# FFN up-projection of a hybrid attention layer: two blocks of one feature group through seven products instead of eight

## The chip, the core and the metric

The kernel runs on one NeuronCore of one Trainium2 chip. The metric is the device time of one execution in microseconds (us), the median of several runs. Five engines work side by side, each with its own in-order queue: TensorE (PE; its weight loads are the row PEld) multiplies, ScalarE (ACT) and VectorE (DVE) cast, copy and add, GpSimd (POOL) does small work, and SyncE (SP) issues the transfers from main memory. They are ordered by semaphores alone: an instruction waits for its operands, and everything queued behind it on its engine waits too.

## What is computed

One layer for 256 tokens of width 2048, in float32. After attention and the first LayerNorm the token matrix `x` (256 x 2048) is modulated by a vector that depends on the condition `c`, goes through a SwiGLU of hidden width 5632, and is added back:

```python
sh1, sc1, g1, sh2, sc2, g2 = ada_mods(c, w_ada, b_ada)          # c (1 x 2048) @ w_ada (2048 x 12288)
x = layer_norm(DN_ALPHA * x + g1 * (heads @ w_out), ln1_g, ln1_b)
u = x * (1.0 + sc2) + sh2
y = (silu(u @ w_gate) * (u @ w_up)) @ w_down                    # 2048 x 5632 twice, 5632 x 2048
x = layer_norm(DN_ALPHA * x + g2 * y, ln2_g, ln2_b)
```

The change lies in `u @ w_gate` and `u @ w_up`.

## The kernel before

**Precision.** A float32 product is made of three matmuls (`mm3`): every operand is split into a high part `hi` (a cast, on ACT) and a rest `lo` (a subtraction, on DVE), and hi\*hi + hi\*lo + lo\*hi is summed in a PSUM bank. Weights arrive in tiles `raw` of 128 partitions x 2048 (four 128-feature slices of 512 columns, 1 MiB), of which there are four (`RAW_BUFS`). Each raw is split in two **pieces** of 128 x 1024 (`hi` and `lo`, four buffers each, `HL_BUFS`); a piece normally feeds 12 matmuls (2 slices, 2 token tiles, 3 terms). A cast into a buffer waits until the piece four before it has been multiplied, so at most three pieces are ready ahead of TensorE.

**Blocks.** The 5632 hidden columns are 11 blocks `f` of 512. The features are four groups `g` of 512. Group 2 (features 1024 to 1535) of the gate columns of blocks 0 to 9 already goes through seven products instead of eight (the Winograd form of Strassen's scheme, `folded`): with half-matrices b11, b21 (one column block) and b12, b22 (the other), DVE forms b12-b11, b22-b12, b22-b11 and b21 of the last of these, and seven products of 6 matmuls each replace eight. A pair of blocks is the pair of columns there. Partial results are handed from bank to bank by ACT copies (`nc.scalar.copy(b, a)` and the like), since three sums share a beginning.

**First half.** The modulation vectors of the groups 1 to 3 need rows of `w_ada`. The kernel starts the FFN before they are there: `first_half` is a list of steps, one for each block, matrix (gate, up) and group, that a call of `project` makes: load a raw, split it, 24 matmuls into two banks. Blocks 0 to 2 do group 0 alone, blocks 3 to 9 groups 0 and 1; when both are in, ACT copies the two banks to SBUF (`spills[f]`). Beside these steps runs `side`, the sums over `w_ada` for groups 2 and 3: 16 steps, each loading 1 MiB of `w_ada` into a raw of the same four and adding it up with two DVE instructions (`adav`, L466). At the end of each group DVE transposes and folds the sum (`flip`, `fold`), TensorE multiplies it by a small matrix (`grp`, L1160), and DVE copies the answer out (`sh`, `sc`). `merge` spreads the 16 side steps evenly over the 25 steps of the list. After the list `z_part` makes the features 1024 to 2047 of `u` (`u2h`, `u2l`), and the second half begins. Outside a small region the order of instructions on each engine is set when the kernel is built, by the program's order and a scheduler.

Of the kernel before, what the change touches and what calls it, by code (L numbers as in the profile page):

```python
# [13 lines left out]
F32 = mybir.dt.float32  # L14
F32R = mybir.dt.float32r
# [251 lines left out]
def dit_layer(ctx: ExitStack, tc: tile.TileContext, x, c, cx, c_ctx, w_ada, b_ada, w_in, q_norm_g,  # L267
# [12 lines left out]
    def acc_bank():  # L280
        return acc_ps.tile([P, NB], F32, tag="acc", name="acc")

    def wk_bank():
        return wk_ps.tile([P, NB], F32, tag="wk", name="wk")

    def run(steps):
        for s in steps:
            s()

    def merge(*lists):  # L290

# [1171 lines left out]
    u2h = pb.tile([P, KD, SEQ], F32R, tag="u2h", name="u2h")  # L1463
    u2l = pb.tile([P, KD, SEQ], F32R, tag="u2l", name="u2l")
    rests = {(t, kk): pb.tile([P, 2, SEQ], F32, tag="t2k", name="uf2", bufs=4)[:, :, :P] for t in range(NT) for kk in (0, 2)}
    hTh = [pb.tile([P, 4, SEQ], F32R, tag=f"hTh{f}", name="hTh") if f < KF // 4 - SPLIT_F else None for f in range(KF // 4)]
    hTl = [pb.tile([P, 4, SEQ], F32R, tag=f"hTl{f}", name="hTl") if f < KF // 4 - SPLIT_F else None for f in range(KF // 4)]

    def z_part(kk, uf=None):
        ps = wk_bank()  # L1470
        for j in range(2):
            for t in range(NT):
                nc.tensor.transpose(ps[:, (j * 2 + t) * P : (j * 2 + t + 1) * P],
                                    xt[:, t, (kk + j) * P : (kk + j + 1) * P], ident)
# [27 lines left out]
    def sums(a11, a21, a12, a22):  # L1502

        tt = nc.vector.tensor_tensor
        tt(a22, a21, a22, op=ALU.add)
        tt(a21, a11, a21, op=ALU.subtract)
        tt(a11, a22, a11, op=ALU.subtract)
        tt(a12, a12, a11, op=ALU.subtract)

    def form_tiles():  # L1510
        return [pb.tile([P, 2, SEQ], F32R, tag="t2k", name=name, bufs=4) for name in ("fh", "fl")]

    def plain(forms, h, l, k0):
        for m, (t, k) in {11: (0, k0), 12: (0, k0 + 2), 22: (1, k0 + 2)}.items():
            forms[m] = [tuple(u[:, k + j, t * P : (t + 1) * P] for u in (h, l)) for j in range(2)]
        return forms

    def token_forms(v1, v2, k0):

        forms = {}  # L1520
        sums(v1[:, :, :P], v1[:, :, P:], v2[:, :, :P], v2[:, :, P:])
        for lr, x in (((2, 3), v1), ((4, 1), v2)):
            hi, lo = form_tiles()
            split(hi, lo, x)
            for i, m in enumerate(lr):
                forms[m] = [(hi[:, j, i * P : (i + 1) * P], lo[:, j, i * P : (i + 1) * P]) for j in range(2)]
        return plain(forms, u2h, u2l, k0)
# [10 lines left out]
                forms[m] = [(hi[:, j, i * P : (i + 1) * P], lo[:, j, i * P : (i + 1) * P]) for j in range(2)]  # L1538
        return plain(forms, hTh[f], hTl[f], 0)

    def folded(columns, forms, shared):


        def products(ps, m, piece, first):
            w = split_raw(piece)
            for j in range(2):
                mm3(ps, *forms[m][j], w[j], first and j == 0, j == 1, not first)

        half = 2 * NB
        r1, r2 = (load_raw(w_, k0, G4, c0, NB) for w_, k0, c0 in columns)  # L1550
        b11, b21, b12, b22 = r1[:, :half], r1[:, half:], r2[:, :half], r2[:, half:]
        a, e = wk_bank(), wk_bank()
        tt = nc.vector.tensor_tensor
        products(a, 11, b11, True)
        b = acc_bank()
        nc.scalar.copy(b, a)
        tt(b11, b12, b11, op=ALU.subtract)
        yield
        products(e, 1, b11, True)
        tt(b12, b22, b12, op=ALU.subtract)  # L1560
        tt(b11, b22, b11, op=ALU.subtract)
# [76 lines left out]


    groups = [1 if f < ONE_F else EARLY_G if f < SPLIT_F else 0 for f in range(FFN // NB)]  # L1640
    spills, first_half = [], []
    for f in range(SPLIT_F):
        spills.append([pb.tile([P, NT, NB], F32, tag=f"hT{c}{KF // 4 - SPLIT_F + f}", name="spill") for c in "hl"])
        for i, w_ in enumerate((w_gate, w_up)):
            st = {}

            def step(g, f=f, i=i, w_=w_, st=st):
                if g == 0:
                    st["accs"] = [acc_bank() for _ in range(NT)]
                project(st["accs"], w_, f, g, 0, groups[f] * 4 - 1)  # L1650
                if g == groups[f] - 1:
                    for t in range(NT):
                        nc.scalar.copy(spills[f][i][:, t, :], st["accs"][t])

            first_half += [lambda g=g, step=step: step(g) for g in range(groups[f])]
    late_sums = [lambda: vector_sums(2 * NB), lambda: pb.tile([P, 2 * NB], F32, tag="lgb", name="adav")]
    scales = ada_vector_steps((4 * D + NB,), NB, lambda: late_sums[1]()[:, :NB], second_scales)
    side = sum((second_modulation(g, late_sums[g - EARLY_G]) for g in range(EARLY_G, ng)), [])
# [78 lines left out]
    for f0 in range(0, SPLIT_F, 2):  # L1737
# [248 lines left out]
```

## Time and profile before

| | |
|---|---|
| Device time, three runs | 1122.33, 1124.48, 1124.83 us (median 1124.48) |
| Profiled execution: span from the first to the last instruction | 1121.0 us (its own device time is not given beside the span; the runs' median is 3.5 us above it) |
| PE busy | 1102.3 us, 98% of the span |
| DVE busy | 903.4 us, 81% |
| ACT busy | 598.7 us, 53% |
| DMA engines | about 82% of the span, 287 GB/s on average |

A busy share is the time in which the engine had an instruction in flight. Matmuls overlap, so a PE that is 100% busy is read by the distance of the starts of two matmuls and not by the length of one.

### The profile page before, as it was taken

The page shows a single profiled execution, that of the slowest core. Times are in us where ns is not written, and L with a number is a line of the kernel's source. Part 1 is how long each engine was busy: PE and PEld are TensorE (multiplying, and loading weights), DVE is VectorE, ACT ScalarE, POOL GpSimd, SP SyncE. Part 2 cuts the span into 40 slices and gives each one's busy share as a digit, 9 for nine tenths or more (in the row PEclk, how much of TensorE's full clock was granted, in tenths as well). Part 3 has the DMA queues.
Part 4 walks back from the last instruction along what each step waited for, and adds up shares of the span by engine and source line. Part 5 has one row for each costly group of instructions (what it writes and reads, how often), then busy time and mean ns, then how long its engine had stood idle before and what let it go on. Part 6 is the DMA issues. An engine that isn't in the chain of part 4 may idle for free.

```text
span 1121.0 us, 14130 instructions
## 1 busy us (share of the span) xinstructions
PE 1102.3 (98%) x5213; PEld 883.7 (79%) x5213; DVE 903.4 (81%) x1133; ACT 598.7 (53%) x875; POOL 36.7 (3%) x82
## 2 busy tenths in 40 slices
PE   8999999999999999999999999999999999999995
PEld 6766688777887788888888878888888888888884
DVE  5763589899999888787778697988996987689876
ACT  3341554878685356444475565767766344444442
POOL 1000030110100001000000000000000000000000
PEclk9999999999999999999999999999999999999998
DMA  9999999778999778999956677777776998669742
GB/s 321 394 385 375 393 362 377 247 234 274 345 332 395 249 269 321 348 318 296 336 182 216 223 220 266 234 246 271 228 267 216 329 348 293 228 235 379 287 149 76
DMA packets 178317, 321.26 MB, mean 287 GB/s; under 512 B 8732, under 2 KB 43196, under 8 KB 175943
## 3 DMA queue, kind: packets, MB, share of 16 engines
q1 hardware_dynamic: 177528, 320.03, 81.7%
q8 instruction: 41, 0.67, 0.2%
q10 hardware_dynamic: 720, 0.33, 0.1%
q14 instruction: 28, 0.23, 0.1%
HBM read 304.07 MB, written 16.25 MB: 286 GB/s over the span
## 4 chain that ended last, share of the span: by engine, by line
PE 91%; DMA 3%; DVE 2%; ACT 1%; SPq 1%; issue 0%; ACTq 0%; DVEq 0%
PE acc L341 20%; PE acc L343 20%; PE acc L342 20%; PE wk L342 8%; PE wk L341 8%; PE wk L343 8%; PE wk L1081 2%; PE wk L654 2%; DMA raw<-in_w_in_dram 2%; DVE lo L332 1%; DMA lgb<-in_ln_g_dram 1%; PE wk L755 1%; SPq L569 1%; DMA xt<-in_x_dram 0%; PE wk L1414 0%
## 5 line engine op out<-in xcount | busy, mean ns | idle before, releaser
L331 ACT CAST hi<-raw 128x1024 fp32r<-128x1024 f32 x279 | 290.7, 1054 | 256.4 <-PE acc L343 162.4
L332 DVE TENSOR_TENSOR lo<-raw,hi 128x1024 fp32r<-128x1024 f32 x279 | 336.1, 1220 | 103.6 <-ACT hi L331 101.4
L341 PE MATMUL acc<-hi,u2h 128*128 128x512 f32 x390 | 152.5, 391 | 0.0
L343 PE MATMUL acc<-hi,u2l 128*128 128x512 f32 x390 | 151.7, 390 | 0.7 <-DVE u2l L1669 0.7
L342 PE MATMUL acc<-lo,u2h 128*128 128x512 f32 x390 | 151.8, 389 | 0.0
L603 ACT CAST hi<-raw 128x1024 fp32r<-128x1024 f32 (+1 forms) x86 | 87.4, 1030 | 113.8 <-DMA raw<-in_w_in_dram 63.2
L466 DVE SCALAR_TENSOR_TENSOR adav<-raw,cs,adav 128x512 f32<-128x512 f32 (+1 forms) x128 | 121.4, 949 | 8.4 <-DMA raw<-in_w_ada_dram 4.9
L606 DVE TENSOR_TENSOR lo<-raw,hi 128x1024 fp32r<-128x1024 f32 (+1 forms) x86 | 101.3, 1194 | 16.3 <-ACT hi L603 15.5
L341 PE MATMUL acc<-hi,uh 128*128 128x512 f32 x256 | 103.7, 405 | 1.3 <-ACT uh L769 0.8
L342 PE MATMUL wk<-lo,u2h 128*128 128x512 f32 x264 | 103.1, 390 | 0.5 <-DVE lo L332 0.5
L343 PE MATMUL wk<-hi,u2l 128*128 128x512 f32 x264 | 102.7, 389 | 0.0
L341 PE MATMUL wk<-hi,u2h 128*128 128x512 f32 x264 | 102.2, 389 | 0.0
L342 PE MATMUL acc<-lo,uh 128*128 128x512 f32 x256 | 100.5, 392 | 0.6 <-DVE lo L606 0.6
L343 PE MATMUL acc<-hi,ul 128*128 128x512 f32 x256 | 100.1, 391 | 0.4 <-DVE ul L784 0.4
L341 PE MATMUL acc<-hi,hTh 128*128 128x512 f32 x236 | 92.0, 390 | 0.4 <-ACT acc L1901 0.4
L342 PE MATMUL acc<-lo,hTh 128*128 128x512 f32 x236 | 91.8, 389 | 0.0
L343 PE MATMUL acc<-hi,hTl 128*128 128x512 f32 x236 | 91.8, 389 | 0.0
L343 PEld LDWEIGHTS acc<-hi,u2l 128*128 128x128 f32 x390 | 73.2, 188 | 16.2 <-DVE u2l L1669 1.1
L341 PEld LDWEIGHTS acc<-hi,u2h 128*128 128x128 f32 x390 | 73.2, 188 | 16.1 <-ACT u2h L1668 0.8
L342 PEld LDWEIGHTS acc<-lo,u2h 128*128 128x128 f32 x390 | 73.2, 188 | 15.1
L341 PEld LDWEIGHTS acc<-hi,uh 128*128 128x128 f32 x256 | 48.1, 188 | 19.0 <-issue 5.6
L342 PEld LDWEIGHTS wk<-lo,u2h 128*128 128x128 f32 x264 | 49.5, 188 | 12.0 <-DVE lo L332 1.8
(277 smaller groups left out, 1748.0 us busy)
## 6 DMA issues: line engine op xcount, KB each, us to landing
raw<-in_w_ada_dram SPq DMA_DIRECT2D x70, 1024.0 KB, 7.7
raw<-in_w_gate_dram SPq DMA_DIRECT2D x44, 1024.0 KB, 6.7
raw<-in_w_up_dram SPq DMA_DIRECT2D x44, 1024.0 KB, 5.6
raw<-in_w_down_dram SPq DMA_DIRECT2D x44, 1024.0 KB, 5.8
raw<-in_w_ada_dram SPq DMA_DIRECT2D x48, 512.0 KB, 5.9
raw<-in_w_in_dram SPq DMA_DIRECT2D x18, 1024.0 KB, 11.0
raw<-in_w_out_dram SPq DMA_DIRECT2D x16, 1024.0 KB, 6.5
pd<-hx SPq DMA_DIRECT2D x64, 128.0 KB, 3.4
```

Source lines behind the costliest of these rows:

```text
L331: nc.scalar.copy(hi[:, :n], raw[:, s : s + n])
L332: nc.vector.tensor_tensor(lo[:, :n], raw[:, s : s + n], hi[:, :n].bitcast(F32), op=ALU.subtract)
L341: nc.tensor.matmul(ps, lhsT=xh, rhs=w[0], start=first, stop=False, skip_group_check=seeded)
L342: nc.tensor.matmul(ps, lhsT=xh, rhs=w[1], start=False, stop=False, skip_group_check=seeded)
L343: nc.tensor.matmul(ps, lhsT=xl, rhs=w[0], start=False, stop=last, skip_group_check=seeded)
L466: nc.vector.scalar_tensor_tensor(a[:, c : c + piece], raw[:, f : f + piece], cs[:, 4 * (g * (G4 * NB // w) + j) + 2, None], a[:, c : c + p ...
L569: nc.sync.dma_start(room.t, w[k0 * P : (k0 + 1) * P, c0 : c0 + width])
L603: nc.scalar.copy(hl.hi[:, :n], raw.t[:, s : s + n])
L606: nc.vector.tensor_tensor(hl.lo[:, :n], raw.t[:, s : s + n], hl.hi[:, :n].bitcast(F32), op=ALU.subtract)
L654: nc.tensor.matmul(bank.t[32 * j : 32 * j + 32, :width], lhsT=cs[:, 4 * k + 2 - 2 * i : 4 * k + 34 - 2 * i], rhs=raw.t[:, c * width : (c + ...
L755: nc.tensor.transpose(ps.t[:, (j * 2 + t) * P : (j * 2 + t + 1) * P], src, ident)
L1081: nc.tensor.matmul(o_ps.t[:, : 2 * P].rearrange("p (g q) -> p g q", q=32), lhsT=v, rhs=pv[:, k], start=k == 0, stop=k == 3)
```

## The change

In blocks 6 and 8 (`EARLY_F`) group 1 (features 512 to 1023, from slice `FOLD_E` = 4) goes through `folded` with the gate and the up columns of the same block as the pair. `fold_steps(f)` makes seven steps of it: five stages of products (one, one, two, two and one of the seven) and two `own` steps that add group 0 of up and of gate. In the list the first four stages stand in turn with normal steps of other blocks. `halves_of` loads the gate half-matrices of such a pair into two tiles of their own (`half`, 512 KiB each) instead of a raw; the up half-matrices take one raw until the fifth and sixth product have been cast. The sums of token halves that the products need (`token_forms`) are made once. The first half's normal blocks from 4 on take PSUM banks of the pool `wk` instead of `acc`, and the folded products use `acc`. `spread` takes the place of `merge`: it gives a side step out whenever DVE instructions per matmul (the table `load`) fall below their mean.

```diff
+    def spread(steps, extra, load):
+        loads = [load.get(s, (24, 2)) for s in steps]
+        share = (sum(v for _, v in loads) + 2 * len(extra)) / sum(n for n, _ in loads)
+        res, extra, debt = [], list(extra), 0.0
+        for s, (n, v) in zip(steps, loads):
+            res.append(s)
+            debt += n * share - v
+            while extra and debt > 0:
+                res.append(extra.pop(0))
+                debt -= 2
+        return res + extra
...
-        r1, r2 = (load_raw(w_, k0, G4, c0, NB) for w_, k0, c0 in columns)
-        b11, b21, b12, b22 = r1[:, :half], r1[:, half:], r2[:, :half], r2[:, half:]
-        a, e = wk_bank(), wk_bank()
+        b11, b21 = (halves_of if first is acc_bank else halves)(*columns[0])
+        b12, b22 = halves(*columns[1])
+        a, e = first(), wk_bank()
...
-                    st["accs"] = [acc_bank() for _ in range(NT)]
+                    st["accs"] = [acc_bank() if f <= ONE_F else wk_bank() for _ in range(NT)]
...
+    def fold_steps(f):
+        st = {}
+        gate, up = spills[f]
+        def shared(e):
+            nc.scalar.copy(up[:, 0, :], e)
+        def stage(i):
+            if i == 0:
+                st["it"] = folded([(w, FOLD_E, f * NB) for w in (w_gate, w_up)], early, shared, acc_bank)
+            st["banks"] = next(st["it"])
+        def own(i, w):
+            project(st["banks"][i], w, f, 0, None, 3, True)
+            for t in reversed(range(NT)):
+                if i:
+                    nc.vector.tensor_add(up[:, t, :], up[:, 0, :], st["banks"][i][t])
+                else:
+                    nc.scalar.copy(gate[:, t, :], st["banks"][i][t])
+        return [lambda i=i: stage(i) for i in range(5)] + [lambda: own(1, w_up), lambda: own(0, w_gate)]
...
+    for f in reversed(EARLY_F):
+        steps = fold_steps(f)
+        load.update(zip(steps, ((6, 2), (6, 3), (12, 3), (12, 2), (6, 1), (24, 3), (24, 2))))
+        normal = [s for e in range(f) if e not in EARLY_F for s in firsts_of[e]]
+        at = len(normal) - 1
+        rest, AT_F = first_half[at:], at
+        mixed = []
+        for s in steps[:4]:
+            mixed += [s, rest.pop(0)]
...
-    z_part(4)
-    z_part(6)
+    heads = [z_part(kk) for kk in (4, 6)]
+    homes = [[u[:, kk : kk + 2, :] for u in (u2h, u2l)] for kk in (8, 10)]
+    plain(early, u2h, u2l, FOLD_E)
+    first_half[AT_F + 1 : AT_F + 1] = [lambda: early.update(token_forms(*heads, FOLD_E, homes))]
     cutoff = len(first_half) - 2
-    run(merge(first_half[2 * ONE_F + 1 : cutoff], side))
+    run(spread(first_half[2 * ONE_F + 1 : cutoff], side, load))
```

The diff leaves the scheduler's order open; three places of it follow. On TensorE the list of the first half now has 12 matmuls fewer between the first `z_part` and the second half (42 instead of 48 for each of the two blocks); group 2's small product (L1160 before, L1175 now) stands 46 matmuls before the first of the seven products of block 6, whose 6 matmuls are followed at once by a normal piece.

VectorE, where the answer of group 2's small product is copied out (`sh`, `sc`), in the kernel before:

```order
L466 SCALAR_TENSOR_TENSOR adav<-raw,cs,adav 128x1024 x2
L332 TENSOR_TENSOR lo<-raw,hi 128x1024 x2
L1167 COPY sh_147<-wk 128x4
L1168 TENSOR_SCALAR sc_148<-wk 128x4
L332 TENSOR_TENSOR lo<-raw,hi 128x1024
L466 SCALAR_TENSOR_TENSOR adav<-raw,cs,adav 128x1024
L332 TENSOR_TENSOR lo<-raw,hi 128x1024
L466 SCALAR_TENSOR_TENSOR adav<-raw,cs,adav 128x1024
L332 TENSOR_TENSOR lo<-raw,hi 128x1024 x2
```

The same place in the changed kernel; it is now just ahead of block 6's first products (`half` is the gate half-matrix), and the last row's first `lo` belongs to the piece that TensorE multiplies right after the first product:

```order
L1182 COPY sh_147<-wk 128x4
L1183 TENSOR_SCALAR sc_148<-wk 128x4
L347 TENSOR_TENSOR lo<-raw,hi 128x1024
L481 SCALAR_TENSOR_TENSOR adav<-raw,cs,adav 128x1024 x2
L347 TENSOR_TENSOR lo<-raw,hi 128x1024 x2
L481 SCALAR_TENSOR_TENSOR adav<-raw,cs,adav 128x1024
L347 TENSOR_TENSOR lo<-half,hi 128x1024
L481 SCALAR_TENSOR_TENSOR adav<-raw,cs,adav 128x1024
L1587 TENSOR_TENSOR half<-raw,half 128x1024
L1590 TENSOR_TENSOR raw<-raw 128x1024
L481 SCALAR_TENSOR_TENSOR adav<-raw,cs,adav 128x1024 x2
L347 TENSOR_TENSOR lo<-raw,hi 128x1024 x2
```

Between the copies and that piece's `lo` there now stand four `lo`, six `adav` and two differences; before, two `adav` stood among the next four `lo`.

ScalarE at the first half's blocks before, where four casts and two copies of finished banks take turns:

```order
L331 CAST hi<-raw 128x1024 x4
L1653 COPY spill<-acc 128x512 x2
L331 CAST hi<-raw 128x1024 x4
L1653 COPY spill<-acc 128x512 x2
L331 CAST hi<-raw 128x1024 x4
```

And in the changed kernel at block 6's first product (its cast is the first `hi<-half`, and `acc<-acc` is the copy `b` of its bank):

```order
L1684 COPY spill<-wk 128x512
L346 CAST hi<-raw 128x1024
L1684 COPY spill<-wk 128x512
L346 CAST hi<-raw 128x1024
L346 CAST hi<-half 128x1024
L1586 COPY acc<-acc 128x512
L346 CAST hi<-raw 128x1024 x2
L346 CAST hi<-half 128x1024
L346 CAST hi<-raw 128x1024 x2
L1684 COPY spill<-wk 128x512 x2
```

The copy of the first product's bank, which needs that product finished, stands ahead of the casts of the two pieces that TensorE multiplies next. At block 8 the two casts stand ahead of the copy.

SyncE's issues after the first `z_part`, before:

```order
L311 DMA raw<-in_w_up_dram 128x4x512
L456 DMA raw<-in_w_ada_dram 128x2x512 x2
L311 DMA raw<-in_w_up_dram 128x4x512
L311 DMA raw<-in_w_gate_dram 128x4x512
L456 DMA raw<-in_w_ada_dram 128x2x512 x2
L311 DMA raw<-in_w_gate_dram 128x4x512
L456 DMA raw<-in_w_ada_dram 128x2x512 x2
L311 DMA raw<-in_w_up_dram 128x4x512 x2
L456 DMA raw<-in_w_ada_dram 128x2x512 x2
```

and now:

```order
L471 DMA raw<-in_w_ada_dram 128x2x512 x2
L326 DMA raw<-in_w_gate_dram 128x4x512
L471 DMA raw<-in_w_ada_dram 128x2x512 x2
L326 DMA raw<-in_w_up_dram 128x4x512
L471 DMA raw<-in_w_ada_dram 128x2x512 x2
L326 DMA raw<-in_w_gate_dram 128x4x512
L471 DMA raw<-in_w_ada_dram 128x2x512 x2
L326 DMA raw<-in_w_gate_dram 128x4x512
L471 DMA raw<-in_w_ada_dram 128x2x512 x2
```

Up to block 6 a `w_ada` load (two issues of 512 KiB) now follows every weight load; before, it followed about two of three.

## Rows read from the trace of the kernel before

**Rows 1.** The page: span and busy time of the engines.

```profile
span 1121.0 us, 14130 instructions
PE 1102.3 (98%) x5213; PEld 883.7 (79%) x5213; DVE 903.4 (81%) x1133; ACT 598.7 (53%) x875; POOL 36.7 (3%) x82
```

**Rows 2.** Busy time by stretch: dense first steps; before and from block 6's place.

```profile
core 0: us, PE busy (x) PEld busy (x) DVE busy (x) ACT busy (x) POOL busy (x), PEclk, DMA share, GB/s
406.00:436.00 30.00, 30.00 (x143) 24.48 (x142) 28.02 (x31) 17.39 (x24) 3.37 (x4) 1.00 0.98 347
432.00:487.00 55.00, 55.00 (x245) 45.37 (x244) 40.85 (x36) 28.88 (x37) 0.00 (x0) 1.00 0.93 324
487.00:569.00 82.00, 82.00 (x376) 67.39 (x375) 61.55 (x59) 39.41 (x45) 1.64 (x7) 1.00 0.92 310
```

**Rows 3.** Timeline of PE in the first half: start, length (us).

```profile
446.20 0.39 PE L342 MATMUL acc<-lo,u2h 128*128 128x512 f32 x1
...
449.15 0.39 PE L343 MATMUL acc<-hi,u2l 128*128 128x512 f32 x1
```

**Rows 4.** Waits in 431 to 582 us: total, times, longest (us).

```profile
ACT hi L331 <- PE acc L343: 53.8, 35, 2.1
DVE lo L332 <- ACT hi L331: 29.3, 27, 2.0
```

**Rows 5.** Groups by shape, 431 to 582 us: busy, mean ns, idle before.

```profile
L332 DVE TENSOR_TENSOR lo<-raw,hi 128x1024 fp32r<-128x1024 f32 x54 | 65.8, 1220 | 29.4 <-ACT hi L331 29.3
L331 ACT CAST hi<-raw 128x1024 fp32r<-128x1024 f32 x54 | 56.8, 1056 | 56.3 <-PE acc L343 53.8 <-DMA raw<-in_w_up_dram 1.3 <-DVE adav L466 1.2
L1653 ACT COPY spill<-acc 128x512 f32<-128x512 f32 x27 | 15.9, 589 | 14.8 <-PE acc L343 13.6
```

**Rows 6.** Timeline of DVE: starts of instructions that follow one another.

```profile
444.13 1.28 DVE L466 SCALAR_TENSOR_TENSOR adav<-raw,cs,adav 128x1024 f32<-128x1024 f32 x1
445.32 1.22 DVE L332 TENSOR_TENSOR lo<-raw,hi 128x1024 fp32r<-128x1024 f32 x1
...
448.79 2.60 DVE L466 SCALAR_TENSOR_TENSOR adav<-raw,cs,adav 128x1024 f32<-128x1024 f32 x2
451.31 1.22 DVE L332 TENSOR_TENSOR lo<-raw,hi 128x1024 fp32r<-128x1024 f32 x1
...
580.34 1.22 DVE L1557 TENSOR_TENSOR raw<-raw 128x1024 f32<-128x1024 f32 x1
581.48 2.35 DVE L332 TENSOR_TENSOR lo<-raw,hi 128x1024 fp32r<-128x1024 f32 x2
```

**Rows 7.** Timeline of PE at group 2's small product.

```profile
497.75 0.25 PE L1160 MATMUL wk<-fold,grp 128*32 128x8 f32 x8
497.93 0.50 PE L341 MATMUL acc<-hi,u2h 128*128 128x512 f32 x1
```

**Rows 8.** Timeline of DVE at the same place.

```profile
498.06 0.16 DVE L1167 COPY sh<-wk 128x4 f32<-128x4 f32 x1 [0.61 <-PE wk L1160]
```

**Rows 9.** Timeline of ACT at a bank copy of the folded products.

```profile
583.63 0.58 ACT L1556 COPY acc<-wk 128x512 f32<-128x512 f32 x1
584.14 1.04 ACT L331 CAST hi<-raw 128x1024 fp32r<-128x1024 f32 x1
```

**Rows 10.** Waits of PE over the whole span, the folded second half included.

```profile
PE wk L342 <- DVE lo L332: 0.5, 2, 0.4
```

**Rows 11.** Busy time by stretch, a dense earlier one (DMA share, GB/s last).

```profile
100.00:140.00 40.00, 39.44 (x231) 24.66 (x229) 18.58 (x25) 16.73 (x24) 0.00 (x0) 1.00 1.04 397
```

**Rows 12.** Loads of weights in 420 to 570 us, by their source line.

```profile
DMA to landing us min/median/max: 5.1/5.9/7.4
```

**Rows 13.** Timelines of PE and ACT at the second `z_part`s.

```profile
569.20 1.91 PE L1473 MATMUL wk<-ident,xt 128*128 128x128 f32 x16
...
569.88 1.48 ACT L1478 ACTIVATE ufs<-wk,mB,mA 128x256 f32<-128x256 f32 x3
```

**Rows 14.** Granted clock where PE is idle after its last matmul, and around short idles.

```profile
1110.00:1121.00 11.00, 0.22 (x1) 0.00 (x0) 6.93 (x14) 2.58 (x10) 0.00 (x0) 0.63 0.33 122
260.00:300.00 40.00, 38.51 (x178) 31.63 (x177) 37.77 (x69) 27.34 (x60) 5.31 (x13) 1.00 0.92 315
```

More of the change, by code (lines that the diff above doesn't have):

```diff
@@ L51 @@
 FOLD_K = 8
+FOLD_E = 4
+EARLY_F = (6, 8,)
 FOLD_H = 6
@@ L1465, in dit_layer @@
     rests = {(t, kk): pb.tile([P, 2, SEQ], F32, tag="t2k", name="uf2", bufs=4)[:, :, :P] for t in range(NT) for kk in (0, 2)}
-    hTh = [pb.tile([P, 4, SEQ], F32R, tag=f"hTh{f}", name="hTh") if f < KF // 4 - SPLIT_F else None for f in range(KF // 4)]
-    hTl = [pb.tile([P, 4, SEQ], F32R, tag=f"hTl{f}", name="hTl") if f < KF // 4 - SPLIT_F else None for f in range(KF // 4)]
+    hTh, hTl = [None] * (KF // 4), [None] * (KF // 4)
+    halves0 = [pb.tile([P, 2 * NB], F32, tag=f"hT{c}0", name="half") for c in "hl"]
     def z_part(kk, uf=None):
@@ L1481, in z_part @@
         nc.vector.tensor_tensor(u2l[:, kk : kk + 2, :], uf, u2h[:, kk : kk + 2, :].bitcast(F32), op=ALU.subtract)
+        return uf
     def residual_base(n):
@@ L1516, in plain, with token_forms @@
         return forms
-    def token_forms(v1, v2, k0):
+    def token_forms(v1, v2, k0, tiles=None):
         forms = {}
+        tiles = tiles or [form_tiles() for _ in range(2)]
         sums(v1[:, :, :P], v1[:, :, P:], v2[:, :, :P], v2[:, :, P:])
-        for lr, x in (((2, 3), v1), ((4, 1), v2)):
-            hi, lo = form_tiles()
+        for lr, x, (hi, lo) in (((2, 3), v1, tiles[0]), ((4, 1), v2, tiles[1])):
             split(hi, lo, x)
@@ L1539, in hidden_forms, with halves_of, folded @@
         return plain(forms, hTh[f], hTl[f], 0)
-    def folded(columns, forms, shared):
+    def halves_of(w, k0, c0):
+        res = []
+        for i, c in enumerate("hl"):
+            half = halves0.pop(0) if halves0 else pb.tile([P, 2 * NB], F32, tag=f"hT{c}0", name="half")
+            k = k0 + 2 * i
+            nc.sync.dma_start(half.rearrange("p (k n) -> p k n", k=2),
+                              w[k * P : (k + 2) * P, c0 : c0 + NB].rearrange("(k p) n -> p k n", p=P))
+            res.append(half)
+        return res
+    def folded(columns, forms, shared, first=wk_bank):
         def products(ps, m, piece, first):
@@ L1547, in products, with halves @@
                 mm3(ps, *forms[m][j], w[j], first and j == 0, j == 1, not first)
-        half = 2 * NB
-        r1, r2 = (load_raw(w_, k0, G4, c0, NB) for w_, k0, c0 in columns)
-        b11, b21, b12, b22 = r1[:, :half], r1[:, half:], r2[:, :half], r2[:, half:]
-        a, e = wk_bank(), wk_bank()
+        def halves(w_, k0, c0):
+            raw = load_raw(w_, k0, G4, c0, NB)
+            return raw[:, : 2 * NB], raw[:, 2 * NB :]
+        b11, b21 = (halves_of if first is acc_bank else halves)(*columns[0])
+        b12, b22 = halves(*columns[1])
+        a, e = first(), wk_bank()
         tt = nc.vector.tensor_tensor
@@ L1640, in dit_layer @@
     groups = [1 if f < ONE_F else EARLY_G if f < SPLIT_F else 0 for f in range(FFN // NB)]
-    spills, first_half = [], []
+    spills, early, firsts_of = [], {}, {}
     for f in range(SPLIT_F):
         spills.append([pb.tile([P, NT, NB], F32, tag=f"hT{c}{KF // 4 - SPLIT_F + f}", name="spill") for c in "hl"])
+        firsts_of[f] = []
         for i, w_ in enumerate((w_gate, w_up)):
@@ L1653, in step @@
                         nc.scalar.copy(spills[f][i][:, t, :], st["accs"][t])
-            first_half += [lambda g=g, step=step: step(g) for g in range(groups[f])]
+            firsts_of[f] += [lambda g=g, step=step: step(g) for g in range(groups[f])]
+    def fold_steps(f):
[15 more added lines that the diff above has]
+        return [lambda i=i: stage(i) for i in range(5)] + [lambda: own(1, w_up), lambda: own(0, w_gate)]
+    first_half, load = [], {}
+    firsts_of[ONE_F][1:3] = reversed(firsts_of[ONE_F][1:3])
+    for f in range(SPLIT_F):
+        if f not in EARLY_F:
+            first_half += firsts_of[f]
+    AT_F = 0
+    for f in reversed(EARLY_F):
[7 more added lines that the diff above has]
+            mixed += [s, rest.pop(0)]
+        if f + 1 < SPLIT_F and len(rest) > 2:
+            first_half[at:] = mixed + [steps[4]] + steps[5:] + rest
+        else:
+            first_half[at:] = mixed + steps[4:] + rest
     late_sums = [lambda: vector_sums(2 * NB), lambda: pb.tile([P, 2 * NB], F32, tag="lgb", name="adav")]
```

## The prediction

> **What bounds the kernel now.** First the page: TensorE is busy for 1102.3 of 1121.0 us [rows 1], so almost all time that can be won must come out of its instructions, and any new idle time on it is lost. Then the busy time by stretch: in the first half, 432 to 569 us, TensorE is never idle (55.00 of 55, 82.00 of 82), while DVE has 25% of it free and the DMA engines show 0.92 to 0.93 [rows 2]. The timeline of PE gives its pace: thirteen matmuls after 446.20 stands the one of 449.15, so a matmul costs 2.95 / 13 = 0.227 us, although each is 0.39 us long [rows 3]. The waits say what stands behind it: ACT's casts mostly wait for PE to give a buffer back (53.8 us), DVE's `lo` for ACT's cast (29.3 us) [rows 4]. Weights are thus split as far ahead as four buffers allow. A piece is cast when the fourth before it is done, that is 3 x 12 x 0.227 = 8.2 us ahead of its use; less 1.06 for the cast and 1.22 for `lo` [rows 5], about 5.8 us of lead remain. This lead is what the change spends.
>
> **What it removes.** Two blocks times (48 - 42) = 12 matmuls, 12 x 0.227 = **-2.7 us** on the path. Nothing else leaves it.
>
> **What it adds off the path.** For each block seven pieces take the place of four: 3 more casts (1.06 each) and 3 more `lo`; 4 differences of 128x1024, which take 1.14 from start to start, as `lo` does [rows 6]; 6 bank copies on ACT in place of 4 (0.59 each [rows 5]); and 2 additions on DVE for up's banks, not in this trace, at most a `lo` each. DVE gets 3 x 1.14 + 4 x 1.14 + 2 x about 0.6 = 9.2 us a block, with the token sums some 21 us in all. It has 137 - 102.4 = 34.6 us free in 432 to 569 [rows 2]. On average it fits, at 92%; the cost is in the order, not in the sum. Taking PSUM banks of the other pool costs nothing where I followed it: a bank is copied out some 6 matmuls before it is written again.
>
> **Where DVE comes late.** DVE's copy of group 2's answer (`sh`) cannot run before TensorE has reached the small product, and all of DVE's queue stands behind it. In the kernel before it started 0.31 us after that product [rows 7, 8] and two plain pieces followed. Now, by the order shown above, there follow up to the `lo` of the piece that TensorE wants right after block 6's first product: four `lo` (4.56), two pairs of `adav` at 2.52 and two single ones at 1.19 [rows 6], two differences (2.28), and that `lo` itself (1.22): 4.56 + 5.04 + 2.38 + 2.28 + 1.22 = 15.5; with 0.31 and 0.2 for the two small copies, 16.0 us after the small product. TensorE wants it 0.18 us [rows 7] and 54 matmuls later (46 to block 6, 6 of the product, 2 that need only `hi`): 12.4 us. Deficit **3.6 us**. Before the small product DVE waits idle, by my reading some 2 us, so nothing earlier can be fetched up.
>
> **Where ACT comes late, at the same place.** The bank copy `b` is queued ahead of the casts of that same piece, and it needs the product finished. From then TensorE has nothing: 0.16 until its last matmul ends (0.39 less 0.227), 0.51 for the copy (583.63 to 584.14 [rows 9]), 1.06 for the cast, 1.22 for `lo`, less 0.45 for two matmuls that run meanwhile: 2.5 us. This is beside the DVE term, not on top of it: the later of the two counts, 3.6, and 2.5 is its lower end even if DVE were on time. At block 8 the casts stand ahead of the copy and DVE has no pair of side steps there, so I take 0.
>
> **Small terms.** The next normal piece after the second product is then about 0.2 us late (difference, `lo` and cast follow at once). At the second `z_part`s two blocks' banks are still held, so the third and fourth transposes wait for ACT to empty the first two; a cast of 1.06 now stands ahead of that work, which began 0.68 us after the transposes before [rows 13]: 0.3 us. The early `half` loads fall where the four raws were not filled, and I take 0, at most the 1.3 us that 512 KiB last at 397 GB/s [rows 11].
>
> **The sum.** -2.7 + 3.6 + 0.2 + 0.3 = +1.4 us: the span goes from 1121.0 to 1122.4. The runs' median is 3.5 us above the span of the profile; I add the difference to it: 1124.5 + 1.4 = **1125.9 us**, 0.12% more. 0.2%, 2.25 us, is about what a measurement of this kernel can tell from no change.
>
> **Transfers, weighed.** `spread` puts a `w_ada` load behind each weight load up to block 6: 2.1 MB for 24 matmuls (5.44 us), 385 GB/s, where the stretch moved 324. The kernel did 397 GB/s over 40 us in an earlier stretch [rows 11], but with the same four raws only 347 at 0.98 busy in 406 to 436 [rows 2]. At 397 it holds. At 347 a step takes 6.04 us, 0.6 too long; over nine steps 5.4 us, against about 2.5 us by which a transfer lands before its use and some 2.3 us of `lo` lead left at the small product: 0.6 us late. I take 0 for the sum and keep the slower end as a rival.
>
> The Trainium skill (DMA: Bandwidth & Descriptors, Specifications) sets an HBM limit of about 358 GB/s per core; the trace's 397 disagrees for a core that runs alone, and by the page the steps would be 0.4 us too long, 3.8 in all, still inside those margins.
>
> **Rivals.** (1) Only ACT's floor is paid, because DVE gets ahead: 2.5 instead of 3.6 and no follower, so -2.7 + 2.5 + 0.3 = +0.1, 1124.6. For it: DVE lengths here were read with few semaphores between them. Against: in-order DVE has idle time only before `sh`. (2) Faster: no wait appears, 1124.5 - 2.7 = 1121.8. For it: the same seven products run in the second half, and over the whole span PE waits for `lo` only 0.5 us [rows 10]. Against: there the next casts are queued ahead of the bank copy. (3) Slower by transfers: the loads run at 320 GB/s, as the stretch did [rows 2]; a step then takes 6.55, 1.1 too long, ten over nine steps, less 4.8 of margins: 5 us, with the smaller of these 3 us beside the main case, 1129. It decides from about 350 GB/s down. For it: the long landings, up to 7.4 us [rows 12]; against: these were queued, not slow. (4) Slower by the clock: a single idle of 3.6 us lets TensorE fall from 2.4 to 1.2 GHz. The profile shows 0.63 granted in the last 11 us, with one matmul in it, and 1.00 around idles of 1.5 us in sum [rows 14]; none is as long as 3.6. If it ran at half pace for as long as it had stood, half of 3.6 us is lost: +1.8, 1127.7.
>
> The Trainium skill (TensorE: Matmul & The Clock Gate, Part 1) says that an idle array falls to the lower level and needs sustained work to leave it; no row here shows it within the work.
>
> **How the numbers follow.** Main case 0.50 (its own range 1124.3 to 1127.5), rival 1 0.17, rival 2 0.10, rival 3 0.15, rival 4 0.08. Faster by over 0.2% is rival 2 with a little of rival 1's lower edge, 0.12. Slower by over 0.2% (from 1126.7) is rivals 3 and 4 and the main case's upper edge, 0.30. The rest, 0.58, is within 0.2%. The range goes from 1122.8, short of rival 2, to 1129.0, with rival 3's size.
>
> **What would show it.** Right: in the after profile PE idle of 3 to 4 us at one place, some 55 us after the first `z_part`, its releaser DVE's `lo` (or ACT's `hi`), directly after six matmuls of the first folded product, with DVE busy without a break from `sh` to there; 12 fewer matmuls; the second half starting 1 to 2 us later. Wrong: PE 100% busy through 432 to 566 (rival 2); an idle in 440 to 480 whose releaser is a DMA of `w_ada` or weights (rival 3); PEclk under 1.00 after the idle (rival 4). The forecast fails if DVE does not stand behind `sh`, if a wait at block 8 as large as block 6's appears, or if the extra casts push the second `z_part`s later than 0.3 us.

## The result, and the profile after

The changed kernel takes 1128.05 us (median of 6 runs, 1126.80 to 1130.19); the kernel before, run beside it on the same chip, 1123.40 (6 runs, 1120.38 to 1124.83). The ratio is 1.0050 (95% interval 1.0038 to 1.0063, that is 4.3 to 7.1 us more). The time lies in the forecast range, but the forecast was "within 0.2%", and that was wrong: the change is slower by more than 0.2%.

The page of the changed kernel, with the lines that answer to [rows 1], and the granted clock in 40 slices of the span:

```profile
span 1127.9 us, 14155 instructions
...
PE 1103.0 (98%) x5201; PEld 883.3 (78%) x5201; DVE 923.8 (82%) x1157; ACT 605.7 (54%) x887; POOL 41.0 (4%) x82
...
PEclk9999999999999999989999999999999999999998
```

There are 12 matmuls fewer (5213 to 5201), yet TensorE is busy 0.7 us longer and one slice of the clock has fallen to 8: the 18th of 40, 479 to 508 us. The busy time by stretch, beside [rows 2], and then around that place:

```profile
core 0: us, PE busy (x) PEld busy (x) DVE busy (x) ACT busy (x) POOL busy (x), PEclk, DMA share, GB/s
432.00:487.00 55.00, 53.53 (x246) 43.50 (x245) 46.80 (x49) 27.28 (x36) 4.07 (x4) 1.00 0.96 342
487.00:576.00 89.00, 85.37 (x371) 69.54 (x370) 75.42 (x69) 48.08 (x56) 0.55 (x3) 0.96 0.76 263
...
496.00:500.00 4.00, 3.53 (x8) 2.81 (x9) 4.00 (x5) 0.00 (x0) 0.00 (x0) 0.50 0.87 307
```

So TensorE, never idle there before, misses 1.47 and 3.63 us in these two stretches, and the clock is at 0.50 from 496 to 500 us. The timeline of PE (start, length, then the idle time before it and what ended it) shows where; its first and last row below are the transposes that open the first and the second `z_part`s:

```profile
432.80 1.03 PE L1488 MATMUL wk<-ident,xt 128*128 128x128 f32 x8
...
482.87 0.39 PE L358 MATMUL wk<-hi,u2l 128*128 128x512 f32 x1
484.20 0.73 PE L356 MATMUL wk<-hi,u2h 128*128 128x512 f32 x2 [0.94 <-ACT hi L346]
485.46 0.50 PE L357 MATMUL wk<-lo,u2h 128*128 128x512 f32 x1 [0.53 <-DVE lo L347]
...
491.72 0.39 PE L358 MATMUL acc<-hi,u2l 128*128 128x512 f32 x1
493.72 0.73 PE L356 MATMUL wk<-hi,u2h 128*128 128x512 f32 x2 [1.62 <-ACT hi L346]
496.47 0.80 PE L357 MATMUL wk<-lo,u2h 128*128 128x512 f32 x1 [2.01 <-DVE lo L347]
497.06 0.63 PE L358 MATMUL wk<-hi,u2l 128*128 128x512 f32 x1
...
501.33 0.63 PE L357 MATMUL wk<-lo,u2h 128*128 128x512 f32 x1
...
502.05 0.40 PE L356 MATMUL wk<-hi,u2h 128*128 128x512 f32 x1
...
576.63 1.03 PE L1488 MATMUL wk<-ident,xt 128*128 128x128 f32 x8
```

Three losses can be read off, each from start to start, less the matmuls between at 0.227 [rows 3]:

- near 484: 485.46 - 482.87 - 3 x 0.227 = **1.9 us**, not in the prediction;
- near 492, after block 6's first product: 496.47 - 491.72 - 0.68 = **4.1 us**, forecast as 3.6 at this very place;
- after it the matmuls last 0.63 and stand 0.427 apart. Thirteen steps take 5.58 us where 2.95 would do: **2.6 us**. The granted clock is 0.50 there, the lower of TensorE's two levels (1.2 GHz).

With -2.7 for the 12 matmuls these make +5.9. The stretch from the first `z_part` to the second, in which the programs differ, went from 569.20 - 431.34 = 137.86 to 143.83 us: +6.0. So the account closes. Below, "the stretch" is this one: TensorE's work ahead of it is the same in all kernels, but the executions reached it at times from 431.3 to 438.7 us, so the stretch tells small things better than the whole time. It is one execution of each kernel; the median and the ratio are of several.

What TensorE waited for, on ACT and on DVE (timelines of the same execution):

```profile
482.62 0.59 ACT L1684 COPY spill<-wk 128x512 f32<-128x512 f32 x1 [8.12 <-PE wk L358]
483.10 1.05 ACT L346 CAST hi<-raw 128x1024 fp32r<-128x1024 f32 x1
...
492.14 0.57 ACT L1586 COPY acc<-acc 128x512 f32<-128x512 f32 x1 [5.61 <-PE acc L358]
492.62 2.00 ACT L346 CAST hi<-raw 128x1024 fp32r<-128x1024 f32 x2
```

```profile
478.11 0.16 DVE L1182 COPY sh<-wk 128x4 f32<-128x4 f32 x1 [1.97 <-PE wk L1175]
...
484.18 1.23 DVE L347 TENSOR_TENSOR lo<-raw,hi 128x1024 fp32r<-128x1024 f32 x1 [2.19 <-ACT hi L346]
485.61 1.23 DVE L347 TENSOR_TENSOR lo<-raw,hi 128x1024 fp32r<-128x1024 f32 x1 [0.21 <-ACT hi L346]
...
492.68 2.60 DVE L481 SCALAR_TENSOR_TENSOR adav<-raw,cs,adav 128x1024 f32<-128x1024 f32 x2
495.20 2.35 DVE L347 TENSOR_TENSOR lo<-raw,hi 128x1024 fp32r<-128x1024 f32 x2
```

Twice ACT stands idle for 5 to 8 us in front of a bank copy that needs TensorE to finish, with the casts that TensorE needs next queued behind the copy. In the kernel before, at the end of a group, ACT had a cast of the next step done before the copies:

```profile
478.82 1.05 ACT L331 CAST hi<-raw 128x1024 fp32r<-128x1024 f32 x1 [1.66 <-PE acc L343]
480.86 1.27 ACT L1653 COPY spill<-acc 128x512 f32<-128x512 f32 x2 [0.98 <-PE acc L343]
```

### The profile page after: what moved, and what is told of

It reads as the page before. It is cut to its first block, busy times and chain, and to the rows that moved or that the text cites. A ratio compares the mean times of both kernels' runs of the same rounds, so it can differ in the third digit from the quotient of the medians.

```text
span 1127.9 us, 14155 instructions
## 1 busy us (share of the span) xinstructions
PE 1103.0 (98%) x5201; PEld 883.3 (78%) x5201; DVE 923.8 (82%) x1157; ACT 605.7 (54%) x887; POOL 41.0 (4%) x82
## 4 chain that ended last, share of the span: by engine, by line
PE 91%; DMA 4%; DVE 2%; ACT 1%; issue 1%; SPq 0%; ACTq 0%; DVEq 0%
PE acc L356 18%; PE acc L358 18%; PE acc L357 18%; PE wk L357 10%; PE wk L358 10%; PE wk L356 10%; PE wk L1096 2%; DMA raw<-in_w_in_dram 2%; PE wk L669 2%; DVE lo L347 1%; DMA raw<-in_w_up_dram 1%; PE wk L770 1%; DMA xt<-in_x_dram 0%; ACT hi L346 0%; DMA raw<-in_w_ada_dram 0%
## 5 line engine op out<-in xcount | busy, mean ns | idle before, releaser
L357 PE MATMUL wk<-lo,u2h 128*128 128x512 f32 x396 | 156.0, 394 | 2.7 <-DVE lo L347 2.7
L356 PE MATMUL wk<-hi,u2h 128*128 128x512 f32 x396 | 154.1, 392 | 2.6 <-ACT hi L346 2.6
L358 PE MATMUL wk<-hi,u2l 128*128 128x512 f32 x396 | 155.2, 392 | 0.0
L358 PE MATMUL acc<-hi,u2l 128*128 128x512 f32 x254 | 99.1, 390 | 0.7 <-DVE u2l L1743 0.7
L356 PE MATMUL acc<-hi,u2h 128*128 128x512 f32 x254 | 99.6, 392 | 0.0
L357 PE MATMUL acc<-lo,u2h 128*128 128x512 f32 x254 | 99.0, 390 | 0.0
L357 PEld LDWEIGHTS wk<-lo,u2h 128*128 128x128 f32 x396 | 75.0, 189 | 20.0 <-DVE lo L347 4.4
L356 PEld LDWEIGHTS wk<-hi,u2h 128*128 128x128 f32 x396 | 74.7, 189 | 19.0 <-ACT hi L346 3.4
L358 PEld LDWEIGHTS wk<-hi,u2l 128*128 128x128 f32 x396 | 75.1, 190 | 15.4
L358 PEld LDWEIGHTS acc<-hi,ul 128*128 128x128 f32 x256 | 48.1, 188 | 11.1 <-DVE ul L799 0.7
```

The costliest lines, as they stand in the source:

```text
L356: nc.tensor.matmul(ps, lhsT=xh, rhs=w[0], start=first, stop=False, skip_group_check=seeded)
L357: nc.tensor.matmul(ps, lhsT=xh, rhs=w[1], start=False, stop=False, skip_group_check=seeded)
L358: nc.tensor.matmul(ps, lhsT=xl, rhs=w[0], start=False, stop=last, skip_group_check=seeded)
```

## Experiments

All edits are to the changed kernel. The table gives the stretch of each profiled execution, the median, and the ratio to the kernel before on the same chip. The letters A to E are the rival causes that each expectation names; A is the one held likeliest when it was written, so what it says changes from one to the next.

| kernel | stretch, us | median, us | ratio (95%) |
|---|---|---|---|
| before | 137.86 | 1122.73 to 1123.40, by chip | 1 |
| changed | 143.83 | 1128.05 | 1.0050 (1.0038 to 1.0063) |
| e1_fill | 141.41 | 1125.58 | 1.0024 (1.0015 to 1.0033) |
| e2_block8 | 145.18 | 1129.29 | 1.0052 (1.0039 to 1.0065) |
| e3_sh_later | 143.94 | 1128.33 | 1.0044 (1.0030 to 1.0058) |
| e4_block6 | 139.12 | 1126.38 | 1.0026 (1.0013 to 1.0040) |
| e5_casts_first | 140.28 | 1125.67 | 1.0019 (1.0006 to 1.0031) |
| e6_side_later | 138.18 | 1123.41 | 1.0004 (0.9991 to 1.0016) |
| e7_all_three | 136.28 | 1121.49 | 0.9985 (0.9976 to 0.9995) |
| e8_block8_casts_first | 141.50 | 1126.78 | 1.0033 (1.0020 to 1.0045) |
| e9_merge | 137.28 | 1122.74 | 0.9999 (0.9989 to 1.0009) |
| e10_without_sh_later | 136.16 | 1121.51 | 0.9987 (0.9978 to 0.9996) |

**e1_fill: does the clock cost anything by itself?**

```
+        if first is acc_bank and not filled:
+            filled.append(1)
+            xh = forms[12][0][0]
+            for _ in range(16):
+                nc.tensor.matmul(e, lhsT=xh, rhs=u2h[:, 0:2, :], start=True, stop=True)
         products(e, 1, b11, True)
```

> The changed kernel with 16 extra matmuls into the bank of the small shared product, ahead of block 6's second product; the bank is overwritten by that product, so they only occupy TensorE. In the order they stand where it idles: 12 (2.7 us at 0.227) in the stall of 3.6 us near 492, 4 (0.9 us) in the one of 1.5 us near 484. No useful work changes. Theory A (the clock fell because TensorE stood still, and that costs about 2.4 us on top of the stall): granted clock 1.00 from 488 to 505, the matmuls after the stall 0.227 apart, time 2.4 us under the changed kernel, 1.0028 of the kernel before. Theory B (the slow matmuls after the stall only follow late operands, the clock costs nothing): time as the changed kernel, 1.005, the matmuls after the gap still 0.4 apart.

PE's timeline and the busy time of this run:

```profile
491.48 2.88 PE L1595 MATMUL wk<-u2h 128*128 128x512 f32 x12
...
495.91 0.50 PE L357 MATMUL wk<-lo,u2h 128*128 128x512 f32 x1 [1.10 <-DVE lo L347]
496.25 0.39 PE L358 MATMUL wk<-hi,u2l 128*128 128x512 f32 x1
496.48 0.40 PE L357 MATMUL wk<-lo,u2h 128*128 128x512 f32 x1
```

```profile
496.00:500.00 4.00, 4.00 (x18) 3.29 (x19) 4.00 (x4) 0.03 (x1) 0.00 (x0) 1.00 0.99 337
```

The wanted matmul starts as late as in the changed kernel (from the last of the product, 491.25, to 495.91 is 4.66 us against 4.75), but the clock stays at 1.00 and the next matmuls are 0.23 apart. The stretch is 2.4 us shorter, the time 2.5. Theory A: the fall of the clock costs 2.4 us here, and it came from TensorE standing still, since work that serves nothing took it away. The Trainium skill (TensorE: Matmul & The Clock Gate, Part 1) says that an idle array falls to the lower level and comes back only with sustained work; the changed kernel's trace agrees, with 0.50 granted from 496 to 500 us, right behind the idle.

**e2_block8 and e4_block6: one block alone.** `EARLY_F = (8,)` and `EARLY_F = (6,)`.

> Only block 8 through seven products, block 6 as before. Theory A (the loss is made at block 6, by DVE's queue behind sh and what follows from it): no idle above 0.5 us between 432 and 566, clock 1.00 there, 6 matmuls fewer are 1.4 us, 0.3 to 0.5 given back at the second z_part: 1.0 us faster, 0.9991 of the kernel before. Theory C (the loads and the extra DVE work cost wherever they stand, half of the loss per block): 2 to 3 us slower than the kernel before, 1.002.

> Only block 6 through seven products, block 8 as before. Theory A: both stalls stay (1.5 and 3.6 us, the clock's 2.4 behind them), only 6 matmuls (1.4 us) are saved and 0.3 us is given back at the second z_part: 6 us slower than the kernel before, 1.0055. Theory C: half of the changed kernel's loss, 1.0025.

PE's timeline with block 8 alone, and its clock:

```profile
534.31 0.73 PE L356 MATMUL wk<-hi,u2h 128*128 128x512 f32 x2 [1.62 <-ACT hi L346]
535.57 0.61 PE L357 MATMUL wk<-lo,u2h 128*128 128x512 f32 x1 [0.53 <-DVE lo L347]
545.02 0.50 PE L356 MATMUL acc<-hi,u2h 128*128 128x512 f32 x1 [2.57 <-ACT hi L346]
```

```profile
534.00:538.00 4.00, 3.17 (x8) 2.24 (x9) 3.71 (x4) 3.09 (x4) 0.00 (x0) 0.73 0.17 47
...
546.00:550.00 4.00, 4.00 (x12) 3.18 (x11) 2.44 (x3) 1.53 (x2) 2.45 (x3) 0.57 0.40 100
```

PE's timeline with block 6 alone, and ACT's and DVE's:

```profile
490.32 0.39 PE L358 MATMUL acc<-hi,u2l 128*128 128x512 f32 x1
492.33 0.73 PE L356 MATMUL wk<-hi,u2h 128*128 128x512 f32 x2 [1.62 <-ACT hi L346]
493.59 0.51 PE L357 MATMUL wk<-lo,u2h 128*128 128x512 f32 x1 [0.53 <-DVE lo L347]
493.93 0.40 PE L358 MATMUL wk<-hi,u2l 128*128 128x512 f32 x1
```

```profile
490.75 0.57 ACT L1586 COPY acc<-acc 128x512 f32<-128x512 f32 x1 [6.62 <-PE acc L358]
491.23 2.00 ACT L346 CAST hi<-raw 128x1024 fp32r<-128x1024 f32 x2
...
492.31 2.36 DVE L347 TENSOR_TENSOR lo<-raw,hi 128x1024 fp32r<-128x1024 f32 x2 [2.10 <-ACT hi L346]
```

Neither theory holds for both runs. I had put the loss down to block 6's place, so block 8 alone should have won 1 us: it lost 5.8 (by the ratio), at a place where the changed kernel has no idle at all. Block 6 alone lost less than half of what A wanted, since neither the idle near 484 nor the clock's fall came. C, half of the loss for each block, met the time of block 6 alone (1.0026 for 1.0025), but block 8 alone cost as much as both together (1.0052). What is common to both is the pair 1.62 and 0.53 behind copy `b`: 493.59 - 490.32 - 0.68 = 2.6 us. That is the floor that the prediction had worked out as 2.5 for ACT alone, and here DVE was waiting for ACT (2.10 us in block 6's case, 1.98 in block 8's). It names a new theory: the loss follows the place of bank copies in ACT's queue, which came out differently in each of these builds, and not the block.

**e3_sh_later and e5_casts_first: a late load, or ACT's order?** The idle near 484 had two explanations. Either the weights that are cast there came late (I took them for those of the load issued at 479.50, when the `lo` behind `sh` gave its raw back), or the cast stood behind a bank copy.

```
             ps = folded_columns(sb, 8)
...
+            def place():
+                nc.vector.tensor_copy(sh2[:, ks, 0], ps[:, 0:4])
...
+            if g == EARLY_G:
+                later.append(place)
...
+    side[8] = lambda s=side[8]: (s(), later.pop(0)())
```

> The changed kernel with the copies sh and sc of group 2 issued one side step later, so that in DVE's queue the lo of the second piece of block 5's gate stands ahead of them. Theory A1 (the stall near 484 comes from the raw buffer that this lo gives back, and so from a load issued only at 479.5): the load goes out about 2 us earlier, the stall of 1.5 us near 484 is gone, the one near 492 shrinks by 1.2 us to ACT's floor of 2.5, the clock's loss with it to about 1.7: 3 us under the changed kernel, 1.0023 of the kernel before. Theory A2 (the stall near 484 comes from ACT's copies of block 5's banks, which stand ahead of the casts): that stall stays at 1.5 us, only the one near 492 shrinks: 1.0037.

```
+    def behind(cast):
+        while held:
+            copy = held.pop(0)
+            with tc.issue_after(cast.ins):
+                copy()
...
-        nc.scalar.copy(b, a)
+        if first is acc_bank:
+            held.append(lambda: nc.scalar.copy(b, a))
...
-                        nc.scalar.copy(spills[f][i][:, t, :], st["accs"][t])
+                        copy = lambda t=t: nc.scalar.copy(spills[f][i][:, t, :], st["accs"][t])
+                        if f > ONE_F:
+                            held.append(copy)
...
```

(`split_raw` calls `behind` with its last cast, and `issue_after` queues the held copies behind that on ACT.)

> The changed kernel with ACT's order mended at both stalls: the bank copies (L1684 spill and L1586 b) are issued behind the casts of the step that follows, all else as it was; DVE's order is the same. Theory A (ACT's order is the whole cause, and DVE comes late near 492 only because it waited 2.2 us for ACT near 484): the idle near 484 is gone, DVE is 2.2 us earlier, the idle near 492 goes from 3.6 to 1.4 us and the clock stays at 1.00: the stretch from the first to the second z_part takes 137.9 - 2.7 + 1.6 = 136.8 us, 0.9992 of the kernel before. Theory D (DVE's queue is late by itself: the load that the cast near 484 needs is issued only at 479.5, when lo behind sh gives its raw back): some 1 us stays near 484 and 3 to 3.6 near 492, the clock falls again: stretch 142 to 143.5, 1.004.

In e3_sh_later that load went out 2 us earlier (477.45 for 479.50) and nothing followed: the idle near 484 stayed, and so did the one near 492, at 1.62 and 1.98 us, which both theories wanted 1.2 us shorter. PE's timeline:

```profile
484.48 0.73 PE L356 MATMUL wk<-hi,u2h 128*128 128x512 f32 x2 [0.94 <-ACT hi L346]
```

The run does not decide what it was meant to decide, since it moved another load. By the semaphores in the changed kernel's trace, the instruction that waits for the load of 479.50 is DVE's first difference of block 6 (L1587); the cast at 483.10 waits for the load issued at 470.02, which landed at 477.4, 5.7 us ahead. So the trace itself rules a late load out near 484.

In e5_casts_first the first idle is gone altogether; this is all that is left between the `z_part`s:

```profile
491.08 0.39 PE L367 MATMUL acc<-hi,u2l 128*128 128x512 f32 x1
493.89 0.73 PE L365 MATMUL wk<-hi,u2h 128*128 128x512 f32 x2 [2.42 <-ACT hi L354]
495.30 0.58 PE L366 MATMUL wk<-lo,u2h 128*128 128x512 f32 x1 [0.68 <-DVE lo L355]
```

So near 484 it was ACT's order alone. Near 492 neither theory was right in full: with ACT mended 495.30 - 491.08 - 0.68 = 3.5 us stay. The rest of the stretch (140.28 against 137.86 - 2.7 + 3.5 = 138.7) is 1.6 us of clock. DVE and ACT of this run, from `sh` to the pieces wanted there:

```profile
479.52 0.16 DVE L1191 COPY sh<-wk 128x4 f32<-128x4 f32 x1 [1.22 <-PE wk L1184]
...
494.03 2.35 DVE L355 TENSOR_TENSOR lo<-raw,hi 128x1024 fp32r<-128x1024 f32 x2
...
492.79 1.99 ACT L354 CAST hi<-raw 128x1024 fp32r<-128x1024 f32 x2 [6.55 <-DVE adav L490]
```

DVE's queue is late by itself: from `sh` on it never waits, and the `lo` that TensorE wants ends at 494.03 + 1.22 = 495.25. But a load is nearly as late. The cast's own weights were issued at 485.69, when a `lo` gave their raw back, and by the trace's semaphores landed at 492.7, just ahead of the cast; the `adav` that the profile names ended at the same moment. The cast was done at 493.8, 0.2 us before DVE came free, so that load by itself would have cost almost the same. How the 3.5 us divide between the side steps' sums on DVE and their loads is not shown.

**e6_side_later: fewer side steps ahead of block 6.** This takes six sums out of DVE's queue there, and their loads with them.

```
+QUIET = (0, 1, 2)
...
+    mix = spread(first_half[2 * ONE_F + 1 : cutoff], side, load)
+    moved = [mix.pop(mix.index(s)) for s in side[9:12]]
+    for s, step in zip(moved, QUIET):
+        mix.insert(mix.index(firsts_of[7][step]) + 1, s)
+    run(mix)
```

> The changed kernel with three of group 3's side steps (the second to the fourth) moved from around the start of block 6 to behind the first three steps of block 7, so that 6 adav sums of 1.26 us (7.6 us) no longer stand in DVE's queue there; in ACT's order the casts of the next piece then stand ahead of copy b by themselves. Theory A and D alike: the idle near 492 is gone and the clock's loss with it, the one near 484 stays (1.5 us idle, 1.8 start to start): stretch 137.9 - 2.7 + 1.8 = 137.0, 0.9992 of the kernel before. Rival E (the 16 side steps with the extra DVE work don't fit whatever their order): the idle moves to 500 to 560, stretch 140 or more, 1.002 or more.

```profile
483.18 0.73 PE L357 MATMUL wk<-hi,u2h 128*128 128x512 f32 x2 [0.94 <-ACT hi L347]
...
534.08 0.50 PE L358 MATMUL wk<-lo,u2h 128*128 128x512 f32 x1 [0.39 <-DVE lo L348]
```

As expected the idle near 492 and the clock's loss are gone and the one near 484 stays. The stretch is 1.2 us longer than forecast, 0.55 of it at a small wait at block 8 (534.08 - 533.30 - 0.227) and 0.3 at another near 541: an idle that has moved on, as rival E had it, but far from the 3 us that E wanted. The ratio can't be told from 1. ACT's order changed too, as the expectation says: the casts came to stand ahead of copy `b`. The pair that holds that order fixed is e5_casts_first against e10_without_sh_later below, where moving the same steps takes the stretch from 140.28 to 136.16 us.

**e7_all_three and e10_without_sh_later: all waits taken away.** e7 joins e3, e5 and e6; e10 leaves out e3's edit.

> The changed kernel with the side steps moved as in the run before, ACT's casts ahead of the bank copies, and sh and sc one side step later: every wait that the trace showed at blocks 5 and 6 taken away at its source. Theory A or D: no idle over 0.3 us between the z_parts, clock 1.00, stretch 137.9 - 2.7 = 135.2 us, 2.7 us faster than the kernel before, 0.9976. Rival E: idle elsewhere in the stretch, 1.000 or slower.

> The version with side steps moved and casts first, but sh and sc back in their place. By e3_sh_later, in which moving sh alone left both idles as they were, it is not needed: no idle over 0.6 us, stretch 136.3 as with it, 0.9985. If sh does matter once ACT is on time, up to 1.2 us come back near 484: stretch 137.5, 0.9995.

The only idle over 0.15 us that is left between the `z_part`s in e7 (in e10 it is 0.39, at 532.45); the expectation had none over 0.3:

```profile
534.24 0.50 PE L367 MATMUL wk<-lo,u2h 128*128 128x512 f32 x1 [0.52 <-DVE lo L356]
```

Both beat both kernels: 1121.49 us against 1122.99 of the kernel before on the same chip (e7) and 1121.51 against 1122.73 (e10), with intervals that leave 1 out, and 1.6 and 1.7 us in the stretch. That fits the prediction's 2.7 for the 12 matmuls, less two small waits, 0.7 near 534 and 0.4 near 541. `sh`'s place doesn't matter.

**e8_block8_casts_first: ACT's order at block 8.** e5's edit with `EARLY_F = (8,)`.

> Block 8 alone with copy b behind the casts of the next step; the bank copies of block 7's last step stay ahead of the casts behind them. With block 8 alone the stretch was 145.2 us, with idles of 1.62 and 0.53 near 534 (copy b, then cast, then lo), one of 2.57 near 545, and a granted clock of 0.73 and 0.57 after them. Theory A (there DVE had time, its lo waited 1.98 us for ACT): the two idles near 534 and the clock's fall behind them go, those near 545 stay: stretch 137.9 - 1.4 + 2.7 + 1.7 = 141 us, 1.0025 of the kernel before. Theory D (a late DVE): no change, 145, 1.005.

```profile
534.43 0.50 PE L366 MATMUL wk<-lo,u2h 128*128 128x512 f32 x1 [0.36 <-DVE lo L355]
542.28 0.50 PE L365 MATMUL acc<-hi,u2h 128*128 128x512 f32 x1 [2.56 <-ACT hi L354]
```

Theory A, nearly to the number (141.5 for 141): with two casts ahead of copy `b`, 0.36 us is left of the idle near 534 (1.62 and 0.53), and the granted clock from 534 to 538 is 1.00 (0.73). The copies of block 7's banks were left ahead of the casts behind them, and the idle there (2.57, now 2.56) is unchanged.

**e9_merge: what upset ACT's order?** `merge` in place of `spread`, nothing else.

> The changed kernel with merge in place of spread for the 16 side steps, as the kernel before has it: the seven products of both blocks stay, only the side steps stand otherwise (by count of steps, so fewer of them ahead of block 6 and more among its products). In ACT's order a cast then stands ahead of the bank copies at the end of block 5's gate, and two ahead of copy b; DVE has sh of group 2 behind block 6's first products. Theory A (spread crowds loads and sums ahead of block 6, this makes the casts late and puts the copies ahead of them): no idle near 484 and 492, clock 1.00, stretch 135.2 plus at most 1 us elsewhere, 0.998. Rival E (the side steps among the products make DVE late there instead): idle of 2 us or more between 490 and 560, stretch 138 or more, 1.000 or slower.

```profile
538.33 0.73 PE L356 MATMUL wk<-hi,u2h 128*128 128x512 f32 x2 [0.26 <-ACT hi L346]
539.59 0.50 PE L357 MATMUL wk<-lo,u2h 128*128 128x512 f32 x1 [0.53 <-DVE lo L347]
```

Both idles are gone, so it was the order that `spread` gives which made them. That it does so by crowding the side steps ahead of block 6 is shown for the idle near 492 (e5 against e10) and argued for the one near 484, which stayed in e6. The stretch is 0.6 us shorter than before, the time can't be told from it: about 2 us come back as four small waits near 538 to 571, the last of them 0.31 for group 3's fold on DVE. Theory A forecast at most 1 us of these, so a stretch of 136.2, rival E one idle of 2 or more and 138: 137.28 lies between them.

## Why the prediction was wrong

**Removed work: right.** 12 matmuls at 0.227 are 2.7 us, and e10 has 1.7 of them in the stretch with 1 us in two known small waits.

**"Where DVE comes late": right in place and mechanism, 4.1 for 3.6.** The idle stood behind block 6's first product, 14 us after group 2's small product, with DVE busy without a break but for two waits (2.19 and 0.21). Moving three side steps removed it (e6; e5 against e10). The chain took 18.6 us instead of 16.0 because of those two waits, and TensorE came 1.9 us later too, by the idle near 484. In e5, without these waits, the chain takes 16.05 us (small product at 479.20, `lo` done at 495.25) and the loss is 3.5: the forecast's own sizes. A weight load, which the forecast put at nothing, was then only 0.2 us short of being the bound.

**"Where ACT comes late": right, and too narrow; this step failed.** 2.5 was measured as 2.6 where ACT alone counted (e4). But the prediction looked at copy `b` only and put the other bank copies at nothing ("Taking PSUM banks of the other pool costs nothing where I followed it"): I followed when a bank is written again, and not what is queued on ACT behind the copy that empties it. The two copies of block 5's gate, which stand just above `b` in ScalarE's order ahead of the prediction, each have a cast for its up behind them, as `b` has at block 6. That is 1.9 us near 484, shown by e5 (casts first: gone) and by the load, which had landed 5.7 us before the cast. The other pool itself is not the cause: e5 and e9 take the same banks and have no idle there.

**The clock, left out of the sum: the largest error, and the second step that failed.** Rival 4 named it, with 1.8 us and a chance of 0.08. It came, with 2.6 us in the trace and 2.4 by e1_fill; the slow matmuls went on for 5.6 us, longer than the idle of 3.63 that rival 4 took for their length. I had only one row with a fallen clock, that of the idle end, and took short idles at 1.00 as evidence against; nothing in the trace of before bore on an idle of 3.6 us.

**Transfers, block 8, half loads: 0 as forecast.** 342 GB/s at 0.96 in 432 to 487 and no idle of TensorE with a DMA as its releaser. But e2_block8 and e8 show that the 0 at block 8 hung on ACT's order there and not on the block, and e5 that the transfers had little to spare.

**Small terms.** The 0.2 us behind block 6's second product does not show in the trace. At the second `z_part`s 0.3 was forecast. One wait is seen: the third transposes start 0.42 us after the matmul at 578.43 instead of 0.23, 0.2 us.

Together, up to the second `z_part`s: -2.7 + 3.6 + 0.2 = +1.1 forecast; -2.7 + 1.9 + 4.1 + 2.6 = +5.9 read off, and +6.0 measured for the stretch. Of the 4.8 us between forecast and reading, 2.6 are the clock, 1.9 the copies near 484, 0.5 the longer wait near 492, less the 0.2 that did not come. The time lay in the range by its slower side, which had been drawn for slow transfers; they did not come, so that was luck.

## What to carry to other kernels

On an in-order engine that both empties banks and prepares the next operands, follow what stands behind each emptying copy: it can't start before TensorE has finished, so an operand behind it can cost TensorE the whole chain (here copy, cast, subtraction: 1.9 and 2.6 us). The kernel before had an order that hides this; changes of the work around it lost that order in some of these builds and kept it in others, so say it explicitly (`issue_after`) before judging the change. And allow for the clock when you price a single idle of a few us on TensorE: here 4.1 us of delay cost 2.6 more, while the delay with block 6 alone (2.6 us) cost nothing more.

## What was not expected of the hardware

The clock's fall doesn't follow the idle's length alone. The pair 1.62 and 0.53 us left the clock at 1.00 with block 6 alone and was followed by 0.73 (534 to 538 us) with block 8 alone; idles of 2.56 (e8) and 2.57 (e2) were followed by 0.67 (542 to 546 us) and 0.57 (546 to 550 us). What decides it was not settled here. The fall can also come in code that no edit touched: in the profile of e9_merge the granted clock is 0.93 from 50 to 100 us, where the kernel before has 1.00, behind waits of 1.45 and 0.76 us near 75, and that execution is 5.8 us above its median.
